# Mask and first score tables in SyncE's queue, swapped key halves of pair 0 on VectorE, and the exponential's function table ahead, in a two-layer diffusion step

## The chip, the cores and the metric

The kernel runs on one core of one Trainium2 chip. The time is device microseconds of one execution, the median of three runs. Engine names in the profile: PE is TensorE, DVE is VectorE, ACT is ScalarE, POOL is GpSimd, SP is SyncE, which only issues transfers; SPq and ACTq are issues of transfers by SyncE and by ScalarE.

## The reference

One step of a trunk with two layers, D = 1024, over 512 latent tokens (8 rows of 64) and 128 context tokens. Layer 0 mixes tokens by neighbourhood attention over 16 heads of 64, layer 1 by grouped-query attention; each is followed by a gated ConvFFN with 2816 hidden columns. Norms and adaptive shift, scale and gate stand around all of them. The change lies in layer 0's attention:

```python
qs, ks_, vs = na_qkv(hs, na_w_qkv[i])
...
bias = rpb[:, dr[:, None, :, None], dc[None, :, None, :]].astype(jnp.float32)
s_lat = jnp.where(col_ok[None, None, None, :, None, :], s_lat + bias[None], -jnp.inf)
s_ctx = jnp.einsum('brqhd,bchd->bhrqc', qg, k_ctx).astype(jnp.float32) * scale
s = jnp.concatenate([s_lat.reshape(b, h, rows, GRID_W, n_lat), s_ctx], axis=-1)
p = jax.nn.softmax(s, axis=-1).astype(v.dtype)
```

A latent token sees all 8 rows, 16 columns around its own, with a learned bias by relative position (`rpb`, per head), and the 128 cached context keys.

## The kernel before, in words

The 640 tokens (512 latent, 128 context) stand transposed in `hT`, as a high and a low part. Each weight tile of 512 KB is loaded by SyncE into one of four `wr` buffers, cast by ScalarE to a high part `wh`, and the remainder `wl` is made by VectorE or GpSimd (`wsplit`, L166 to L180); three matmuls, (high, high), (high, low) and (low, high), stand for one in full precision.

Stages at the start: loads, norms and modulation columns; values of heads 0 to 3 (`v_part`, until about 53 us); then queries and keys by pairs of heads. `na_qk_items(p)` gives pair `p` two loads (`load_q`, `load_k`) and 16 `part`s, 8 for queries and 8 for keys, each six matmuls into a bank `qk`. Of a key bank, `k_put` makes for each head of the pair a tile `kh` whose own 64 rows and whose other 64 rows (the swapped half) both hold the high part, and a tile `kl` with the low part in its own rows. `load_q` also loads cached keys `kc`.

`stream()` runs these items one after the other. After 20 parts (`PRO`: pair 0, and the first half of pair 1's queries) the first head is begun. `Head(h)` calls `na_table(h)`: three transfers, issued by ScalarE, fetch runs of the bias into `tr` (one buffer), and GpSimd makes the table `tb` from `mask` and `tr` in three operations. There are two `tb` buffers, for even and odd heads. `scores(slot)` is a pair of matmuls `s`, a VectorE operation that adds the table and finds the extreme `nm`, an exponential on ScalarE into `p`, a reciprocal `rc` on VectorE and a scaling of `p` on GpSimd. `turns` transposes `p` on TensorE (`tp`). Between the scores, further `part`s fill TensorE. `ada_work` streams modulation weights beside it, into two buffers of its own.

A scheduler of the language lays down the order of each engine's stream from the program, and sets semaphores; an engine works its stream in order, so an instruction that waits holds all behind it. Issues of transfers stand in the stream of the engine that issues them. `tc.add_manual_dep(..., no_sync)` fixes an order without a wait; all of TensorE's instructions are chained so (`pe`). A transfer also waits for the one before it on its semaphore, of which there are eight.

Of the kernel before, what the change touches and what calls it, by code (L numbers as in the profile page):

```python
# [19 lines left out]
P = 128  # L20
D = 1024
# [13 lines left out]
RPAD = 32  # L35
RLEN = 15 * 31 + 2 * RPAD
RUN = 8 * 31 + 1
# [35 lines left out]
def raw_ap(ap, offset, dims):  # L73
    return bass.AP(tensor=ap.tensor, offset=ap.offset + offset, ap=[list(d) for d in dims])
# [30 lines left out]
def hybrid_step(ctx: ExitStack, tc: tile.TileContext, A, O):  # L105
    nc = tc.nc
    no_sync = mybir.DependencyInfo(mybir.DependencyClass.NoSync, mybir.DependencyReason.DATA)
# [11 lines left out]
    def turn(*a, **k):  # L119
        pe(nc.tensor.transpose(*a, **k))  # L120

    def f32(t):
        return t.bitcast(F32)

    def pool(name, bufs=1, side="left", **k):
        return tc.tile_pool(name=name, bufs=bufs, side=side, reuse_waits="tile", **k)

    cst = ctx.enter_context(pool("cst"))
    wp = ctx.enter_context(pool("wp", 4))
    sm = ctx.enter_context(pool("sm", 4))  # L130
# [18 lines left out]
    mhalf = cst.tile([P, 1], F32, name="mhalf")  # L149
# [12 lines left out]
    def x_in(t):  # L162
        return A["x_sample"][0, t * P : (t + 1) * P, :] if t < 4 else A["x_prompt"][0]


    def wsplit(src, a, b, low=None, own=None, pin=False, after=None):  # L166
        q = own or wp
        raw = wp.tile([P, a, b], F32, tag="wr", name="wr")
        nc.sync.dma_start(raw, src)
        hi = q.tile([P, a, b], F32R, tag="wh", name="wh")  # L170
        i = nc.scalar.copy(hi, raw)  # L171
        lo = q.tile([P, a, b], F32R, tag="wl", name="wl")
        j = (low or nc.vector).tensor_sub(lo, raw, f32(hi))  # L173
        if after:
            behind(i, after[0])
            behind(j, after[1])
        if pin:
            tc.keep_in_program_order(i)
            tc.keep_in_program_order(j)
        return hi, lo  # L180

    def rows(w, r0, nr, c0, ncol):
        return w[r0 * P : (r0 + nr) * P, c0 : c0 + ncol].rearrange("(k p) n -> p k n", p=P)
# [81 lines left out]
    def ada_work(p, rawp, group, steps, todo, wait=1, sizes=()):  # L265

        bias = p.tile([P, 256], F32, name="abias")
        gr = p.tile([P, 256], F32, name="again")  # L270
        nc.gpsimd.memset(bias, 0.0)
        nc.gpsimd.memset(gr, 0.0)

        def quarters(row):
            return row.rearrange("(j c) -> j c", j=4)

        loads = deque((l, idx, k) for l, idx in todo for k in range(KC))
        raws = deque()

        def load():  # L280
            if loads:
                l, idx, k = loads.popleft()
                raw = rawp.tile([P, D], F32, tag="wr", name="wr")
                nc.sync.dma_start(raw, A["ada_w"][l, k * P : k * P + P, idx * D : idx * D + D])
                raws.append((l, idx, k, raw))

        for _ in range(group):
            load()
        for _ in range(wait):
            yield  # L290
        sizes = iter(sizes)
        while raws:
            n = min(len(raws), next(sizes, len(raws)))
            for _ in range(n):
                l, idx, k, raw = raws.popleft()
                if k == 0:
                    for q in range(2):
                        nc.sync.dma_start(bias[q::32, :], quarters(A["ada_b"][l, idx * D : idx * D + D]))
                        if idx in gain_of:
                            nc.sync.dma_start(gr[q::32, :], quarters(A[gain_of[idx]][l]))  # L300
                    ps = bk.get("ada")
                for j in range(4):
                    mm(ps[32 * j : 32 * j + 32, 0:256], scolp[:, 2 * k : 2 * k + 32], raw[:, 256 * j : 256 * j + 256],
                       start=k == 0, stop=k == KC - 1)
                if k < KC - 1:
                    continue
                orow = p.tile([P, 256], F32, tag="arow", name="arow")
                nc.vector.tensor_add(orow, ps[:, 0:256], bias)
                bk.put(ps)
                if idx in gain_of:  # L310
                    nc.vector.scalar_tensor_tensor(
                        orow, orow, 1.0 if idx in (1, 4) else 0.0, gr, op0=ALU.add, op1=ALU.mult
                    )
                for q in range(2):
                    nc.scalar.dma_start(quarters(modrow[l][idx][q]), orow[q::32, :])
            for i in range(steps):
                for _ in range(n if steps == 1 else i < n):
                    load()
                yield
# [144 lines left out]
    hT = new_hT(r_h0.enter_context(pool("h0", 1, "right")))  # L464
    l_na = ExitStack()
    vpool = l_na.enter_context(pool("nav", 3))
    wqkv = A["na_w_qkv"][0]

    def na_v_tile():
        return vpool.tile([P, 6, 4, HD], F32, tag="vt", name="vt", bufs=2)  # L470

    def na_v_put(vt, c, src):
        nc.scalar.copy(vt[:, c], src.rearrange("p (a d) -> p a d", a=4))

    def na_v_cache(vts, g):
        vc = vpool.tile([P, 256], F32, tag="vc", name="vc", bufs=1)
        nc.scalar.dma_start(
            vc, A["cache_na_v"][0, 0][:, 4 * g : 4 * g + 4, :].rearrange("t h d -> t (h d)")
        )
        na_v_put(vts, 5, vc)  # L480

    def na_v_out(g, src):
# [6 lines left out]
    vts_of, normed = {}, []  # L489
    with ExitStack() as s:  # L490
# [114 lines left out]
        vb = [bk.get("vp") for _ in range(NT)]  # L605
# [39 lines left out]
        v_part(6, range(NT))  # L645
        for c in range(NT):
            v_part(7, (c,))
            na_v_put(vts_of[0], c, vb[c][:, 0:256])
            if c == 4:
                na_v_out(0, vb[c][:, 0:256])  # L650
            bk.put(vb[c])

# [51 lines left out]
            nc.scalar.copy(hi, raw)  # L704
            return nc.vector.tensor_sub(lo, raw, f32(hi))

    def behind(ins, other):
        tc.add_manual_dep(ins.ins, other.ins.name, no_sync, reason="order")

    class Mix:  # L710


# [45 lines left out]

    with l_na:
        ap = l_na.enter_context(pool("na", 2))  # L760
        mask = ap.tile([P, 2, 32, 8], F32, name="mask", bufs=1)
        nc.scalar.dma_start(mask, A["k_mask"])
        tbs = [ap.tile([P, 7, P], F32, name=f"tb{i}", bufs=1) for i in range(2)]
        for tb in tbs:
            nc.gpsimd.memset(tb[:, 3, :], 0.0)
# [33 lines left out]
        def na_qk_items(p):  # L799
            d = {}  # L800

            def load_q():
                d["w"] = wsplit(rows(wqkv, 0, 8, P * p, P), 8, P, nc.gpsimd if p else None, after=None if p else normed)
                kc = ap.tile([P, P], F32, tag="kc", name="kc", bufs=2)
                nc.scalar.dma_start(
                    kc, A["cache_na_k"][0, 0][:, 2 * p : 2 * p + 2, :].rearrange("t h d -> t (h d)")
                )
                d["kc"] = kc

            def load_k():  # L810
                d["wk"] = wsplit(rows(wqkv, 0, 8, 1024 + P * p, P), 8, P, nc.gpsimd if p else None)

            def k_put(c0, c1, src):
                for b in range(2):
                    own, oth = own_oth(b)
                    nc.scalar.copy(d["kh"][b][own, c0:c1], src[own])
                    nc.scalar.copy(d["kh"][b][oth, c0:c1], src[own])
                    nc.vector.tensor_sub(d["kl"][b][own, c0:c1], src[own], f32(d["kh"][b][own, c0:c1]))

            def part(which, half, k0):  # L820
                w = d["w"] if which == 0 else d["wk"]
# [61 lines left out]
            return v6[:, 0:5:2, :] if slot == 0 else v6[:, slot - 1 : slot + 2, :]  # L883

        def na_table(h):
            tr = ap.tile([P, 2, RUN], F32, tag="tr", name="tr", bufs=1)
            base = h * RLEN + RPAD
            for dst, off, n in ((tr[:, 0, :], -8, 16), (tr[0:64, 1, :], 8, 8), (tr[64:128, 1, :], -16, 8)):
                nc.scalar.dma_start(dst, raw_ap(A["k_rpb"], base + off, [[1, n], [31, 8], [1, RUN]]))
            tb = tbs[h % 2]  # L890
            for w, dst in ((1, tb[:, 0::6, :]), (0, tb[:, 1:3, :]), (0, tb[:, 4:6, :])):
                t0 = tr[:, w, :]
                rv = raw_ap(t0, RUN - 1, [t0.ap[0], [-16, 2], [-1, 16], [-31, 8]])
                nc.gpsimd.tensor_sub(
                    dst.rearrange("p c (a b) -> p c a b", b=8),
                    mask[:, w].rearrange("p (c a) b -> p c a b", c=2), rv,
                )
            return tb
# [132 lines left out]
        for h in range(H):  # L1031
            nxt = Head(h + 1) if h + 1 < H else None
            g = h // 4
            pr = h % 4 == 1
            order = (ORDER if h < 13 else ORDER2)[h % 2] if h else ORDER0
            for i, step in enumerate(order):
# [402 lines left out]
    wqkv = A["gqa_w_qkv"][0]  # L1439
# [309 lines left out]
    for hq in range(2):  # L1749
        for n, t in enumerate(((4, 0, 1, 2, 3), (0, 1, 2, 3, 4))[hq]):  # L1750
# [3 lines left out]
            i = 5 * hq + n  # L1754
# [169 lines left out]
```

## Time and profile before

| | us |
|---|---|
| median of three runs | 1574.69 (1573.96 to 1576.03) |
| the profiled execution, its time | 1575.78 |
| its span | 1573.9 |
| PE busy | 1523.1 |
| DVE, ACT, POOL busy | 1029.7, 860.2, 699.5 |
| mean granted clock of PE | 0.99 |

The profiled execution is one run; its time is 1.88 us more than the span that the trace covers. In a row of a timeline stand the start, the duration, engine, line, operation, `out<-in` with sizes, how many (`x2`), and in brackets how long the engine had been idle and what ended it. Rows of waits give who waited for whom, the total in us, the number of times and the longest. Rows by windows give, after the stretch and its length, the busy time of PE, PEld, DVE, ACT and POOL, then the granted clock of PE, the busy share of the transfer engines, and GB/s.

### The profile page before, as it was taken

The numbers are of one execution on the slowest core, as the hardware profiler recorded it, in microseconds if no ns is written. First come the engines' busy times: TensorE is split into PE (matmuls) and PEld (weight loads), VectorE is DVE, ScalarE is ACT, GpSimd is POOL, SyncE is SP. The second block draws the span as 40 slices with busy tenths as digits, with TensorE's granted clock in tenths as the row PEclk, the third lists the DMA queues.
The fourth block names the chain that finished last, engine by engine and source line by source line (L and its number), as shares of the span: only waits on it lengthen the run. The fifth ranks groups of instructions, "written<-read, shape, count | busy, mean of one in ns | idle before, by whom it ended". The sixth has DMA issues, their size and how long they took to land.

```text
span 1573.9 us, 26057 instructions
## 1 busy us (share of the span) xinstructions
PE 1523.1 (97%) x9709; PEld 1351.0 (86%) x9709; DVE 1029.7 (65%) x1654; ACT 860.2 (55%) x1641; POOL 699.5 (44%) x606
## 2 busy tenths in 40 slices
PE   6799999999999999999999999999999999999998
PEld 4789899788999999978887777877899999988886
DVE  4353433649877666856757867773888887786554
ACT  4474655636655555554545436763666665554443
POOL 1455554422355555524444453542325566553433
PEclk9999999999999999999999998999999999999999
DMA  9745454245466665387574211004633334448664
GB/s 296 202 110 144 126 147 120 76 140 168 151 227 186 218 193 153 116 276 267 183 226 148 83 64 49 1 1 156 206 116 114 106 111 150 133 155 270 213 221 135
DMA packets 193211, 242.41 MB, mean 154 GB/s; under 512 B 11101, under 2 KB 149565, under 8 KB 193085
## 3 DMA queue, kind: packets, MB, share of 16 engines
q1 hardware_dynamic: 182224, 233.13, 46.2%
q10 hardware_dynamic: 10860, 7.62, 2.9%
q8 instruction: 76, 1.25, 0.3%
q14 instruction: 51, 0.41, 0.1%
HBM read 214.38 MB, written 26.34 MB: 153 GB/s over the span
## 4 chain that ended last, share of the span: by engine, by line
PE 61%; DVE 7%; ACT 2%; issue 2%; POOL 2%; DMA 2%; ACTq 0%; POOLq 0%; DVEq 0%; SPq 0%
PE acc L117 19%; PE ux L117 18%; PE uz L117 8%; PE uy L117 4%; PE y L117 2%; PE po L117 2%; PE s L117 2%; PE gp L117 2%; PE tp L120 2%; PE ada L117 1%; DMA wr<-in_ffn_w_up 1%; DVE wl L173 1%; DVE t L1244 1%; DMA gn<-in_gqa_k_norm 1%; DVE gkl L1527 1%
## 5 line engine op out<-in xcount | busy, mean ns | idle before, releaser
L173 POOL TENSOR_TENSOR wl<-wr,wh 128x1024 fp32r<-128x1024 f32 x70 | 171.7, 2455 | 237.9 <-ACT wh L171 223.0
L1167 POOL TENSOR_TENSOR wl<-wr,wh 128x1024 fp32r<-128x1024 f32 x76 | 183.4, 2435 | 48.3 <-ACT wh L1166 44.7
L117 PE MATMUL ux<-B,wh 128*128 128x322 f32 x832 | 200.1, 311 | 0.9 <-ACT u L1221 0.9
L1244 DVE SCALAR_TENSOR_TENSOR t<-C,cw,t 128x644 f32<-128x644 f32 x176 | 156.2, 888 | 51.3 <-ACT t L1242 50.7
L117 PE MATMUL acc<-wh,alo 128*128 128x512 f32 x440 | 172.3, 392 | 0.3 <-DVE alo L1136 0.3
L117 PE MATMUL acc<-wl,ahi 128*128 128x512 f32 x440 | 172.0, 391 | 0.0
L117 PE MATMUL acc<-wh,ahi 128*128 128x512 f32 x440 | 171.9, 391 | 0.0
L171 ACT CAST wh<-wr 128x1024 fp32r<-128x1024 f32 x140 | 145.4, 1048 | 43.8 <-DMA wr<-in_ffn_w_down 34.2
L117 PE MATMUL uz<-B,wh 128*128 128x322 f32 x640 | 156.2, 312 | 1.4 <-ACT v L1221 1.4
L117 PEld LDWEIGHTS ux<-B,wh 128*128 128x128 f32 x832 | 143.6, 189 | 3.3 <-ACT u L1221 1.6
L1136 DVE TENSOR_TENSOR alo<-ain,ahi 128x384 fp32r<-128x384 f32 (+1 forms) x88 | 83.9, 973 | 83.1 <-ACT ahi L1134 79.4
L117 PE MATMUL ux<-B,wl 128*128 128x322 f32 x416 | 129.5, 311 | 2.7 <-DVE wl L1167 2.7
L117 PE MATMUL qk<-hT,wh 128*128 128x384 f32 (+1 forms) x512 | 123.7, 318 | 0.0
L117 PEld LDWEIGHTS uz<-B,wh 128*128 128x128 f32 x640 | 110.9, 189 | 4.9 <-ACT v L1221 2.0
L1167 POOL TENSOR_TENSOR vl<-wr,vh 128x1024 fp32r<-128x1024 f32 x38 | 95.9, 2523 | 24.6 <-ACT vh L1166 24.3
L173 DVE TENSOR_TENSOR wl<-wr,wh 128x1024 fp32r<-128x1024 f32 x70 | 92.9, 1338 | 20.7 <-ACT wh L171 20.2
L1166 ACT CAST wh<-wr 128x1024 fp32r<-128x1024 f32 x84 | 84.8, 1049 | 39.7 <-DVE wr L1190 39.4
L1242 ACT ACTIVATE t<-C,cw 128x644 f32<-128x644 f32 x88 | 78.6, 893 | 48.5 <-DVE C L1272 40.9
L117 PE MATMUL uz<-B,wl 128*128 128x322 f32 x320 | 99.6, 311 | 0.3 <-POOL wl L1167 0.3
L117 PEld LDWEIGHTS acc<-wh,alo 128*128 128x128 f32 x440 | 82.5, 188 | 18.8 <-DVE alo L1136 1.1
L117 PEld LDWEIGHTS acc<-wl,ahi 128*128 128x128 f32 x440 | 82.6, 188 | 18.3 <-POOL wl L173 0.4
L117 PEld LDWEIGHTS acc<-wh,ahi 128*128 128x128 f32 x440 | 82.6, 188 | 17.6
(256 smaller groups left out, 3884.9 us busy)
## 6 DMA issues: line engine op xcount, KB each, us to landing
wr<-in_ffn_w_up SPq DMA_DIRECT2D x88, 512.0 KB
wr<-in_ffn_w_down SPq DMA_DIRECT2D x88, 512.0 KB
wr<-in_ada_w SPq DMA_DIRECT2D x72, 512.0 KB
act<-act SPq DMA_DIRECT2D x44, 321.0 KB
wr<-in_na_w_qkv SPq DMA_DIRECT2D x24, 512.0 KB
mod<-modrow SPq DMA_DIRECT2D x20, 512.0 KB
ain<-act SPq DMA_DIRECT2D x44, 192.0 KB
wf<-in_ada_w SPq DMA_DIRECT2D x16, 512.0 KB
```

The lines of the kernel that those rows point to most:

```text
L117: pe(nc.tensor.matmul(*a, **k))
L120: pe(nc.tensor.transpose(*a, **k))
L171: i = nc.scalar.copy(hi, raw)
L173: j = (low or nc.vector).tensor_sub(lo, raw, f32(hi))
L1136: pin(nc.vector.tensor_sub(lo[:, 0 : c1 - c0], ain[:, 0 : c1 - c0], f32(hi[:, 0 : c1 - c0])))
L1166: nc.scalar.copy(hl[0], src)
L1167: low.tensor_sub(hl[1], src, f32(hl[0]))
L1242: nc.scalar.activation(t, taps(0), AF.Identity, bias=cw[:, 3, n : n + 1], scale=cw[:, 1, n : n + 1])
L1244: nc.vector.scalar_tensor_tensor(t, taps(d), cw[:, w, n : n + 1], t, op0=ALU.mult, op1=ALU.add)
L1527: nc.vector.tensor_sub(kl[part, b::2, cols], tv[own], f32(kh[own, b::2, cols]))
```

## The change

Four edits, all around the first two heads.

The mask gets memory of its own from the start (`tpool`, apart from the attention's pool), and is loaded by SyncE behind pair 0's key weights. Tables 0 and 1's runs are loaded behind it by SyncE as well, table 0 into a `tr` buffer of `tpool`, table 1 into one of the four `wr` buffers (`na_runs`). The next three weight loads of SyncE are ordered behind them (`queue`). Table 2's runs, the cached values of the second group and the casts of pair 2's weights are ordered behind the last own-half key copy of pair 0 (`kput`); ScalarE issues runs for heads from 2 on, as before. In `k_put`, for pair 0 alone, VectorE makes the swapped halves in ScalarE's place. A one-element exponential behind the first group's values brings the function table load forward.

```diff
+    queue = []
...
-        nc.sync.dma_start(raw, src)
+        i = nc.sync.dma_start(raw, src)
+        if queue:
+            behind(i, queue.pop())
...
+        if high:
+            behind(i, high[0])
...
+    tpool = l_na.enter_context(pool("nat"))
+    mask = tpool.tile([P, 2, 32, 8], F32, name="mask")
+    kput = []
...
+        if g == 1:
+            behind(i, kput[0])
...
+        behind(nc.scalar.activation(sm.tile([P, 1], F32, name="ss"), mhalf, AF.Exp), i)
...
-        mask = ap.tile([P, 2, 32, 8], F32, name="mask", bufs=1)
-        nc.scalar.dma_start(mask, A["k_mask"])
+        runs = {}
+
+        def na_runs(h, q=nc.scalar):
+            if h == 1:
+                tr = wp.tile([P, 2, RUN], F32, tag="wr", name="tr")
+            else:
+                tr = tpool.tile([P, 2, RUN], F32, tag="tr", name="tr", bufs=1)
+            runs[h] = tr
+            base = h * RLEN + RPAD
+            for dst, off, n in ((tr[:, 0, :], -8, 16), (tr[0:64, 1, :], 8, 8), (tr[64:128, 1, :], -16, 8)):
+                i = q.dma_start(dst, raw_ap(A["k_rpb"], base + off, [[1, n], [31, 8], [1, RUN]]))
+                if h == 2:
+                    behind(i, kput[0])
+            return i
...
-                d["wk"] = wsplit(rows(wqkv, 0, 8, 1024 + P * p, P), 8, P, nc.gpsimd if p else None)
+                d["wk"] = wsplit(rows(wqkv, 0, 8, 1024 + P * p, P), 8, P, nc.gpsimd if p else None, high=kput if p == 2 else None)
+                if not p:
+                    nc.sync.dma_start(mask, A["k_mask"])
+                    for h in range(2):
+                        i = na_runs(h, nc.sync)
+                    queue.extend([i] * 3)
...
-                    nc.scalar.copy(d["kh"][b][own, c0:c1], src[own])
-                    nc.scalar.copy(d["kh"][b][oth, c0:c1], src[own])
+                    i = nc.scalar.copy(d["kh"][b][own, c0:c1], src[own])
+                    (nc.scalar.copy if p else nc.vector.tensor_copy)(d["kh"][b][oth, c0:c1], src[own])
...
+                if not p:
+                    kput[:] = [i]
```

Where it moves instructions. On SyncE, behind the last modulation loads (`wf`), stand before the weights of pair 0 (two) and pair 1 (two), two modulation loads, and pair 2's:

```order
L545 DMA wf<-in_ada_w 128x4x256 x4
L169 DMA wr<-in_na_w_qkv 128x8x128 x4
L284 DMA wr<-in_ada_w 128x1024 x2
L169 DMA wr<-in_na_w_qkv 128x8x128 x2
L298 DMA abias<-in_ada_b 4x256
```

Now:

```order
L561 DMA wf<-in_ada_w 128x4x256 x4
L174 DMA wr<-in_na_w_qkv 128x8x128 x2
L840 DMA mask<-in_k_mask 128x512
L785 DMA tr<-in_k_rpb 128x1x249
L785 DMA tr<-in_k_rpb 64x1x249 x2
L785 DMA tr<-in_k_rpb 128x1x249
L785 DMA tr<-in_k_rpb 64x1x249 x2
L174 DMA wr<-in_na_w_qkv 128x8x128
L293 DMA wr<-in_ada_w 128x1024
L174 DMA wr<-in_na_w_qkv 128x8x128
L293 DMA wr<-in_ada_w 128x1024
L174 DMA wr<-in_na_w_qkv 128x8x128
```

Seven transfers now stand between pair 0's and pair 1's weights, and modulation loads alternate with what follows.

On ScalarE, from pair 0's second query copies (384 columns) to its last key copies (`kh`), a part of the stream before:

```order
L889 DMA tr<-in_k_rpb 128x1x249
L889 DMA tr<-in_k_rpb 64x1x249
L843 ACTIVATE qs_668<-qk 64x64
L889 DMA tr<-in_k_rpb 64x1x249
L843 ACTIVATE qs_669<-qk 64x64
...
L889 DMA tr<-in_k_rpb 128x1x249
L889 DMA tr<-in_k_rpb 64x1x249 x2
L858 COPY kp<-qk 128x128
L816 CAST kh_740<-qk 64x384
L817 CAST kh_740<-qk 64x384
```

The same place now, up to the first exponential `p`:

```order
L848 CAST kh_753<-qk 64x256
L848 CAST kh_753<-tk 64x128
L848 CAST kh_754<-tk 64x128
L848 CAST kh_754<-qk 64x256
L892 COPY kp<-qk 128x128
L848 CAST kh_753<-qk 64x384
L848 CAST kh_754<-qk 64x384
L178 CAST wh<-wr 128x1024
L877 ACTIVATE qs_833<-qk 64x256
L178 CAST wh<-wr 128x1024
L966 ACTIVATE p,su<-s,nm 128x384
```

No `tr` issue is left ahead of the key copies, one copy per head and piece is gone, and the two casts of pair 2's weights stand between the key copies and the first exponential.

On GpSimd, from the clearing of `kl` to the first scalings of `p`, the order before:

```order
L173 TENSOR_TENSOR wl<-wr,wh 128x1024
L271 MEMSET abias 128x256
L272 MEMSET again 128x256
L173 TENSOR_TENSOR wl<-wr,wh 128x1024
L894 TENSOR_TENSOR tb_611<-mask,tr 128x256 x2
L894 TENSOR_TENSOR tb_611<-mask,tr 128x2x128
L173 TENSOR_TENSOR wl<-wr,wh 128x1024
L894 TENSOR_TENSOR tb_612<-mask,tr 128x256 x2
L894 TENSOR_TENSOR tb_612<-mask,tr 128x2x128
L173 TENSOR_TENSOR wl<-wr,wh 128x1024
L894 TENSOR_TENSOR tb_611<-mask,tr 128x2x128
L937 TENSOR_SCALAR p<-p,rc 128x384
```

and now:

```order
L280 MEMSET abias 128x256
L281 MEMSET again 128x256
L927 TENSOR_TENSOR tb_615<-mask,tr 128x2x128
L927 TENSOR_TENSOR tb_615<-mask,tr 128x256 x2
L927 TENSOR_TENSOR tb_616<-mask,tr 128x2x128
L927 TENSOR_TENSOR tb_616<-mask,tr 128x256 x2
L180 TENSOR_TENSOR wl<-wr,wh 128x1024 x4
L970 TENSOR_SCALAR p<-p,rc 128x384 x4
L927 TENSOR_TENSOR tb_615<-mask,tr 128x256 x2
```

Both tables stand ahead of pair 1's `wl`, and the four `wl` of pairs 1 and 2 in a row ahead of the four scalings of head 0. TensorE's order is the same as before.

More of the change, by code (lines that the diff above doesn't have):

```diff
@@ L120, in turn, with behind @@
         pe(nc.tensor.transpose(*a, **k))
+    def behind(ins, other):
+        tc.add_manual_dep(ins.ins, other.ins.name, no_sync, reason="order")
     def f32(t):
@@ L163, in x_in, with wsplit @@
         return A["x_sample"][0, t * P : (t + 1) * P, :] if t < 4 else A["x_prompt"][0]
-    def wsplit(src, a, b, low=None, own=None, pin=False, after=None):
+    queue = []
+    def wsplit(src, a, b, low=None, own=None, pin=False, after=None, high=None):
         q = own or wp
         raw = wp.tile([P, a, b], F32, tag="wr", name="wr")
-        nc.sync.dma_start(raw, src)
+        i = nc.sync.dma_start(raw, src)
+        if queue:
+            behind(i, queue.pop())
         hi = q.tile([P, a, b], F32R, tag="wh", name="wh")
@@ L283, in load @@
                 raw = rawp.tile([P, D], F32, tag="wr", name="wr")
-                nc.sync.dma_start(raw, A["ada_w"][l, k * P : k * P + P, idx * D : idx * D + D])
+                i = nc.sync.dma_start(raw, A["ada_w"][l, k * P : k * P + P, idx * D : idx * D + D])
+                if queue:
+                    behind(i, queue.pop())
                 raws.append((l, idx, k, raw))
@@ L472, in na_v_put @@
     def na_v_put(vt, c, src):
-        nc.scalar.copy(vt[:, c], src.rearrange("p (a d) -> p a d", a=4))
+        return nc.scalar.copy(vt[:, c], src.rearrange("p (a d) -> p a d", a=4))
     def na_v_cache(vts, g):
         vc = vpool.tile([P, 256], F32, tag="vc", name="vc", bufs=1)
-        nc.scalar.dma_start(
+        i = nc.scalar.dma_start(
             vc, A["cache_na_v"][0, 0][:, 4 * g : 4 * g + 4, :].rearrange("t h d -> t (h d)")
         )
+        if g == 1:
+            behind(i, kput[0])
         na_v_put(vts, 5, vc)
@@ L647, in hybrid_step @@
             v_part(7, (c,))
-            na_v_put(vts_of[0], c, vb[c][:, 0:256])
+            i = na_v_put(vts_of[0], c, vb[c][:, 0:256])
             if c == 4:
@@ L705, in split @@
             return nc.vector.tensor_sub(lo, raw, f32(hi))
-    def behind(ins, other):
-        tc.add_manual_dep(ins.ins, other.ins.name, no_sync, reason="order")
     class Mix:
@@ L802, in load_q @@
             def load_q():
-                d["w"] = wsplit(rows(wqkv, 0, 8, P * p, P), 8, P, nc.gpsimd if p else None, after=None if p else normed)
+                d["w"] = wsplit(rows(wqkv, 0, 8, P * p, P), 8, P, nc.gpsimd if p else None, after=None if p else normed, high=kput if p == 2 else None)
                 kc = ap.tile([P, P], F32, tag="kc", name="kc", bufs=2)
@@ L885, in na_table @@
         def na_table(h):
[L886 to L889, printed above, removed]
+            if h not in runs:
+                na_runs(h)
+            tr = runs.pop(h)
             tb = tbs[h % 2]
```

## The prediction, made before the changed kernel ran

> **What bounds the kernel now.** I read the page's shares first, then TensorE's waits over the whole span, then, around the longest wait, the timelines of the engines that it hangs on.
>
> ```profile
> PE 1523.1 (97%) x9709; PEld 1351.0 (86%) x9709; DVE 1029.7 (65%) x1654; ACT 860.2 (55%) x1641; POOL 699.5 (44%) x606
> PE s L117 <- ACT kh L817: 8.6, 1, 8.6
> PE ct L120 <- DMA ident<-in_k_ident: 7.9, 1, 7.9
> ```
>
> TensorE is the bound: it is busy for 97% of the span. Its longest single wait, 8.6 us, is for the first score `s` of the first head, which waits for ScalarE's key copies at L817. The next row is the first transfer of the program. In TensorE's timeline the wait stands between these rows, and the windows show the granted clock (the column after the five engines):
>
> ```profile
> 66.91 0.45 PE L117 MATMUL qk<-hT,wh 128*128 128x384 f32 x2
> 69.83 0.28 PE L117 MATMUL qk<-hT,wh 128*128 128x256 f32 x1
> 78.69 0.69 PE L117 MATMUL s<-kh,qs 128*128 128x384 f32 x1 [8.58 <-ACT kh L817]
> 81.67 0.42 PE L120 MATMUL tk<-ident,kp 128*128 128x128 f32 x1
> 84.36 0.34 PE L117 MATMUL s<-kh,qs 128*128 128x384 f32 x1
> 85.78 0.34 PE L117 MATMUL s<-kh,qs 128*128 128x384 f32 x1
> 70.11:78.69 8.58, 0.00 (x1) 0.01 (x1) 1.89 (x7) 4.38 (x15) 3.79 (x4) 0.73 0.65 107
> 78.69:84.36 5.67, 5.67 (x17) 5.28 (x18) 2.88 (x8) 5.51 (x11) 3.77 (x3) 0.51 0.28 66
> ```
>
> The last key matmul of pair 0 is the first of the two that begin at 66.91. TensorE stops at 70.11 and starts again at 78.69. After the wait it runs 5.67 us at clock 0.51. What ScalarE does meanwhile:
>
> ```profile
> 60.66 2.10 ACTq L889 DMA_DIRECT2D tr<-in_k_rpb  x3
> 63.30 0.49 ACT L843 ACTIVATE qs<-qk 64x384 fp32r<-64x384 f32 x1 [5.72 <-DMA tr<-in_k_rpb]
> 70.39 0.22 ACT L843 ACTIVATE qs<-qk 64x64 fp32r<-64x64 f32 x1 [5.15 <-issue]
> 75.63 1.84 ACTq L889 DMA_DIRECT2D tr<-in_k_rpb  x3
> 77.52 0.27 ACT L858 COPY kp<-qk 128x128 f32<-128x128 f32 x1 [3.29 <-issue]
> 77.68 0.47 ACT L816 CAST kh<-qk 64x384 fp32r<-64x384 f32 x1
> 65.86 1.70 POOL L894 TENSOR_TENSOR tb<-mask,tr 128x256 f32<-128x256 f32 x2 [6.21 <-DMA tr<-in_k_rpb]
> 68.21 0.86 POOL L894 TENSOR_TENSOR tb<-mask,tr 128x256 f32<-128x256 f32 x1 [0.65 <-DMA tr<-in_k_rpb]
> 74.75 0.85 POOL L894 TENSOR_TENSOR tb<-mask,tr 128x256 f32<-128x256 f32 x1 [0.56 <-DVE kl L818]
> ```
>
> ScalarE stands three times (5.72, 5.15, 3.29 us) behind issues of `tr` loads in its own stream. There is one `tr` buffer: table 1's load waits until GpSimd has built table 0 (its last row ends at 69.07), table 2's until table 1 is built (75.60), and the key copies come behind both. The chain is load, build, load, build, copy, with nothing of TensorE in it.
>
> **The change part by part.** It takes those loads out of ScalarE's stream. SyncE issues the mask and tables 0 and 1, table 1 into a weight buffer; table 2's load stands behind the key copies.
>
> *First term: the wait.* ScalarE is then free when the keys come. The last key matmul ends by 67.36 at the latest (66.91 + 0.45); `kp` takes 0.27 and the own half 0.47 (rows above): 68.10. VectorE's swapped half is a form that the trace does not show. Its bounds are the same job on ScalarE, 0.47, and a wider VectorE copy from the same memory, 0.69; the low part behind it is 0.55:
>
> ```profile
> 78.16 0.47 ACT L817 CAST kh<-qk 64x384 fp32r<-64x384 f32 x1
> 78.67 0.55 DVE L818 TENSOR_TENSOR kl<-qk,kh 64x384 fp32r<-64x384 f32 x1 [3.98 <-ACT kh L817]
> 91.84 0.69 DVE L948 COPY pk<-tp 128x512 f32<-128x512 f32 x1
> ```
>
> So `kl` is ready between 69.12 and 69.34, both ahead of 70.11. I take all 8.58 us as gone; the slack is about 0.8 us. The other end is that some of the wait stays (first rival).
>
> *Second term: the low clock.* From 78.69 to 84.36 TensorE runs two rounds of a score pair and six projection matmuls, and one `tk` transposition. The next such round, at full clock, is 85.78 − 84.36 = 1.42 us. At full clock the stretch costs 2 x 1.42 + 0.1 for `tk` (its 0.42 at half clock would be 0.2 at most) = 2.94, so 5.67 − 2.94 = 2.73 us go too if there is no wait. The bounds are 0 (a wait long enough to lower the clock stays) and 2.73; I take 2.73, as the clock was 1.00 until the wait. The Trainium skill, "TensorE: Matmul & The Clock Gate", Part 1, says that the clock halves after an idle window of about 3.4 us and returns after about 3.4 us of work, at a phase that varies; by it this term is an estimate of 1.7 us and the sum would be 1.0 us smaller. Here the low clock lasted 5.67 us, and the measured stretch decides.
>
> *Third term: a new wait, on `tp`.* What is late next is the first transposition of probabilities:
>
> ```profile
> 87.90 1.14 POOL L937 TENSOR_SCALAR p<-p,rc 128x384 f32<-128x384 f32 x2
> 88.63 0.80 PE L120 MATMUL tp<-ident,p 128*128 128x128 f32 x4
> 78.66 1.04 ACT L171 CAST wh<-wr 128x1024 fp32r<-128x1024 f32 x1
> 69.03 2.37 POOL L173 TENSOR_TENSOR wl<-wr,wh 128x1024 fp32r<-128x1024 f32 x1
> ```
>
> `tp` follows the fourth score by 88.63 − 85.78 = 2.85 us, and already waits a little for the fourth `p` (0.80 us for four). It moves to 88.63 − 11.31 = 77.32. On GpSimd four `wl` now stand ahead of the four `p`, and the casts for the last two come behind the key copies. The first cast starts at about 69.6 (the second head's own half waits for the first's `kl`) and ends at 70.6, the second, after a query copy, at 72.0; their `wl` of 2.37 end at 73.0 and 75.4, four `p` of 0.57 at 77.7 to 78.2 (the last one also waits for ScalarE, which issues two table-2 loads of 0.6 us before the last exponential). The fourth transposition would start at 77.6. I take 0.5 us. The bounds are 0 and 2.4 (one `wl` late).
>
> *Terms that I take as zero, and their covers.*
>
> ```profile
> 37.25 8.51 SPq L169 DMA_DIRECT2D wr<-in_na_w_qkv  x4
> 52.07 1.51 SPq L169 DMA_DIRECT2D wr<-in_na_w_qkv  x2
> 40.00:50.00 10.00, 9.17 (x94) 7.56 (x94) 6.09 (x16) 5.32 (x10) 0.00 (x0) 1.00 1.15 282
> tr<-in_k_rpb ACTq DMA_DIRECT2D x16, 124.5 KB
> tr<-in_k_rpb ACTq DMA_DIRECT2D x32, 62.2 KB
> 51.22 3.07 POOL L769 MEMSET kl<- 64x768 f32 x4
> 56.61 0.30 POOL L271 MEMSET abias<- 128x256 f32 x1
> 67.20 0.27 PE L117 MATMUL qk<-hT,wl 128*128 128x256 f32 x1
> 87.30 0.28 PE L117 MATMUL qk<-hT,wl 128*128 128x256 f32 x1
> ```
>
> Seven transfers pass ahead of pair 1's weights in SyncE's queue: the mask (256 KB) and two tables of 249 KB, together 0.75 MB, or 2.7 us at the 282 GB/s of that stretch. Pair 1's query weights, issued within the 8.51 us from 37.25, then land near 53 to 55. On GpSimd their `wl` stands behind six table operations of 0.85: the memsets end at 54.3, the two small ones at 54.9, the tables at 60.0, `wl` at 62.4; TensorE asks for it at 67.20, so 4.8 us of cover. Pair 1's key weights now share a buffer with pair 0's query weights, since table 1 holds one of the four, so their issue moves to 52.07, where such a wait ended before. With 8 us to land, 1.04 and 2.37 they are ready by 65; TensorE asks at 87.30 − 11.31 = 76.0. Without that cover each us late is a us of TensorE.
>
> Table 2, for head 2, comes later than tables 0 and 1: its load is issued near 75.5, lands 5.2 us on (60.66 to 65.86 above), and its three operations, with a `wl` among them, end by 86; head 2's first score moves from 105.90 to 94.6.
>
> ```profile
> 105.90 0.42 PE L117 MATMUL s<-kh,qs 128*128 128x384 f32 x1
> 81.10 1.28 ACT L933 ACT_TABLE_LOAD   x1
> 55.86 0.38 ACT L843 ACTIVATE qs<-qk 64x256 fp32r<-64x256 f32 x1 [2.21 <-PE qk L117]
> 90.00:130.00 40.00, 39.74 (x316) 35.83 (x314) 20.31 (x60) 26.34 (x77) 21.32 (x22) 1.00 0.52 129
> ```
>
> The function table (1.28 us) moves from 81.10, inside the low-clock stretch, to about 53.5, where ScalarE had 2.21 us to spare. Behind it stand the cast and the query copies, wanted only by 70. The six swapped halves are 2.2 us that leave ScalarE for a VectorE that waits there. From 90 to 130 TensorE is busy for 39.74 of 40.00 us and no other engine for more than 26.34, so I expect the shift to carry to the end.
>
> *Sum.* −8.58 − 2.73 + 0.5 = −10.8 us. The profiled execution took 1575.78 us, 1.88 more than its span, and 1.09 more than the median of the three runs. Its span becomes 1563.1, its time 1565.0; against the median the forecast is 1574.69 − 10.8 = 1563.9 us.
>
> **The rivals.** *Part of the wait stays (same sign, smaller).* ScalarE is in order, and the two casts of pair 1's weights stand ahead of the first and second query copies. From the second cast to the last key copy lie some 5.5 us of its work and VectorE's, so from a landing after about 63 on, each us keeps one us of the wait. Against it: issue at 52.07. For it: transfers were saturated at 40 to 50 (share 1.15). With 3 to 5 us kept, the low clock may stay as well: 1567 to 1571 us.
>
> *The gain is given back.* An engine other than TensorE sets the pace of the heads, and the 11 us return as waits before 130: 1574.7 us. Against it are the 39.74 of 40.00 above.
>
> *Slower: weights late behind tables.* GpSimd holds pair 1's `wl` until both tables are loaded and built. If table 1 lands at 71 instead of about 52, its three operations end at 73.6 and `wl` at 76.0; TensorE stands 8.8 us at 67.2 and loses 2.7 more at the low clock, and the gain is used up. If it lands at 76, 13.8 + 2.7 are lost against 11.3, and the time is some 1580 us. For it: table 1's loads wait in a queue that also carries the weights. Against it: a table needed 5.2 us beside two weight loads, and a delay of 19 is asked for. The Trainium skill, "DMA: Bandwidth & Descriptors", Queues, rings and completion order, says that each issuing queue's descriptors are consumed in ring order on the same 16 engines; by that rule weights issued behind the tables land behind them.
>
> **How the numbers follow.** Forecast 0.72 (its own range 1562 to 1566: the sum with 0 to 2.4 for the third term), partial 0.16, given back 0.07, slower 0.05. A measurement of this kernel can tell about 0.2%, 3.1 us. Partial lies past that: faster 0.88, same 0.07, slower 0.05. The range takes in the forecast's and most of the partial case: 1561.8 to 1570.
>
> **What would show it.** TensorE's waits have no row for `s` on `kh` above 1 us; the windows from 70 to 90 show clock 1.00; ScalarE has no `tr` issue between 55 and 70; GpSimd's six table operations lie between 54 and 61; the first `s` starts near 70.1 and `tp` near 77.5 with up to 1 us of wait on `p`. A wait of TensorE at 67 or at 76 on `wl`, or a `CAST` of ScalarE held by a weight load past 63, would make it wrong.

## The result, and the profile after

The changed kernel takes 1567.5 us, median of six runs (1563.37 to 1568.93), against 1574.72 for the kernel before beside it (1573.59 to 1576.03): ratio 0.9948, 95% interval [0.9935, 0.9962]. The forecast was 1563.9 us, faster, range 1561.8 to 1570. The sign and the range held; the median lies above the forecast's own range of 1562 to 1566. The gain is 7.2 us by these medians where 10.8 were forecast, and, as the experiments show, it is made up otherwise than the sum said.

The profiled execution of the changed kernel took 1564.15 us, 1.75 more than its span of 1562.4; it lies 3.35 us under the median. A line of its page, its waits of TensorE (who waits for whom, us in total, times, longest), and one row of the waits of before that the prediction did not use:

```profile
PE 1518.7 (97%) x9709; PEld 1347.9 (86%) x9709; DVE 1028.1 (66%) x1660; ACT 858.4 (55%) x1636; POOL 700.2 (45%) x606
```

```profile
PE ct L120 <- DMA ident<-in_k_ident: 7.3, 1, 7.3
PE tp L120 <- POOL p L970: 4.5, 5, 2.9
PE row L117 <- DMA wf<-in_ada_w: 0.2, 1, 0.2
```

```profile
PE row L117 <- DMA wf<-in_ada_w: 2.6, 4, 0.9
```

The wait of `s` for `kh`, 8.6 us before, has no row any more. A row is new: `tp` waits for GpSimd's `p` (L970 is L937 of before), 2.9 us at once. The wait of the first modulation matmuls (`row`) for `wf`, 2.6 us before, is nearly gone, though no edit touches those transfers. TensorE's timeline of the changed kernel, from the first score `s` to head 1's transpositions:

```profile
66.86 0.34 PE L117 MATMUL s<-kh,qs 128*128 128x384 f32 x1
69.90 0.33 PE L117 MATMUL s<-kh,qs 128*128 128x384 f32 x1
74.16 0.27 PE L120 MATMUL tp<-ident,p 128*128 128x128 f32 x1
75.81 0.42 PE L117 MATMUL s<-kh,qs 128*128 128x384 f32 x1
92.53 0.38 PE L120 MATMUL tp<-ident,p 128*128 128x128 f32 x2
95.85 1.03 PE L120 MATMUL tp<-ident,p 128*128 128x128 f32 x2 [2.94 <-POOL p L970]
96.54 0.67 PE L117 MATMUL s<-kh,qs 128*128 128x384 f32 x1
99.21 0.33 PE L117 MATMUL s<-kh,qs 128*128 128x384 f32 x1
```

The next rows are of the timelines, each kernel's own: first a value matmul at the start and the instructions at the new wait in before, then the same value matmul after:

```profile
43.89 0.39 PE L117 MATMUL vp<-wh,hT 128*128 128x256 f32 x1
105.55 0.60 PE L120 MATMUL tp<-ident,p 128*128 128x128 f32 x4
107.38 0.34 PE L117 MATMUL s<-kh,qs 128*128 128x384 f32 x1
```

```profile
40.79 0.38 PE L117 MATMUL vp<-wh,hT 128*128 128x256 f32 x1
```

TensorE's order is the same in both kernels, so the start of one and the same instruction, after less before, shows where time comes from. The 78.69, 84.36 and 88.63 of before stand in the prediction; 89.18 is the score behind head 0's first `tp`.

| instruction | before | after | difference | what the step is |
|---|---|---|---|---|
| third group of value matmuls | 43.89 | 40.79 | −3.10 | the start |
| first `s`, head 0 | 78.69 | 66.86 | −11.83 | the wait: −8.73 |
| third `s`, head 0 | 84.36 | 69.90 | −14.46 | the low clock: −2.63 |
| first `s`, head 1 | 89.18 | 75.81 | −13.37 | head 0's `tp` wait for `p`: +1.09 (+0.27 in a1_again, below) |
| first `tp`, head 1 | 105.55 | 92.53 | −13.02 | small waits: +0.35 |
| second `s`, head 2 | 107.38 | 99.21 | −8.17 | new: +4.85 |

From there the difference stays between −8.2 and −8.4 us up to 850 us. The windows of the changed kernel (busy time of PE, PEld, DVE, ACT, POOL, then the granted clock, the share of the transfer engines, GB/s) show the last step as a wait with a low clock behind it:

```profile
74.00:90.00 16.00, 15.20 (x112) 13.39 (x111) 8.36 (x25) 11.45 (x31) 7.68 (x9) 1.00 0.64 180
90.00:94.00 4.00, 2.91 (x19) 2.64 (x18) 0.43 (x1) 0.00 (x0) 3.59 (x4) 1.00 0.02 6
94.00:98.00 4.00, 2.06 (x7) 1.77 (x8) 1.72 (x5) 3.12 (x12) 2.58 (x4) 0.72 0.75 111
98.00:102.00 4.00, 4.00 (x29) 3.97 (x28) 2.70 (x8) 3.15 (x7) 3.30 (x4) 0.86 0.34 101
```

What GpSimd, ScalarE and SyncE did meanwhile (their timelines, in that order):

```profile
51.53 5.03 POOL L927 TENSOR_TENSOR tb<-mask,tr 128x256 f32<-128x256 f32 x6
81.57 0.85 POOL L927 TENSOR_TENSOR tb<-mask,tr 128x256 f32<-128x256 f32 x1
90.41 2.53 POOL L927 TENSOR_TENSOR tb<-mask,tr 128x256 f32<-128x256 f32 x3 [6.85 <-DMA tr<-in_k_rpb]
92.90 2.34 POOL L180 TENSOR_TENSOR wl<-wr,wh 128x1024 fp32r<-128x1024 f32 x1
95.21 1.15 POOL L970 TENSOR_SCALAR p<-p,rc 128x384 f32<-128x384 f32 x2
82.45 1.87 ACTq L785 DMA_DIRECT2D tr<-in_k_rpb  x3
94.27 0.27 ACT L903 COPY ko<-tk 128x128 f32<-128x128 f32 x1 [4.85 <-issue]
82.28 1.21 SPq L293 DMA_DIRECT2D wr<-in_ada_w  x2
```

This is table 3, for head 3. Heads from 2 on share one `tr` buffer, so ScalarE issues table 3's runs when table 2's last operation (81.57 + 0.85) is done. In that moment SyncE issues 1 MB of modulation weights. The runs land 6.1 us after their last issue (84.32 to 90.41). GpSimd stands 6.85 us with head 1's last two `p` behind the table in its stream, and ScalarE stands behind table 4's issue. No one needs table 3 yet; TensorE needs the `p`. In before, the three pieces of the same load were issued at 89.62, 90.27 and 93.25, ahead of the modulation weights, and had landed 2.8 us after the last issue (93.85 to 96.69); its timelines of ScalarE, SyncE and GpSimd:

```profile
89.62 0.58 ACTq L889 DMA_DIRECT2D tr<-in_k_rpb  x1
90.27 0.62 ACTq L889 DMA_DIRECT2D tr<-in_k_rpb  x1
93.25 0.60 ACTq L889 DMA_DIRECT2D tr<-in_k_rpb  x1
95.29 0.82 SPq L284 DMA_DIRECT2D wr<-in_ada_w  x2
96.69 0.88 POOL L894 TENSOR_TENSOR tb<-mask,tr 128x256 f32<-128x256 f32 x1 [2.72 <-DMA tr<-in_k_rpb]
```

So table 3's runs were issued 7.2 us (first piece) to 9.5 us (last) earlier than in before and landed 6.3 us earlier, while TensorE came to head 1's `tp` 13.0 us earlier: the loads through the one buffer did not keep up with it. Had the runs landed 2.8 us after their last issue here too, they would have been there 3.2 us sooner, about the length of the wait. That the modulation weights held them is argued from this; no run moved those weights alone.

The last 3 us by which this execution ends ahead (span 1573.9 to 1562.4 is 11.5, not 8.4) come at 880 to 950 us, where TensorE's granted clock falls in some executions and in others not:

```profile
890.00:897.00 7.00, 6.47 (x18) 5.31 (x19) 5.55 (x13) 3.61 (x11) 3.08 (x3) 0.53 0.01 2
```

```profile
882.00:886.00 4.00, 3.61 (x18) 3.06 (x19) 3.85 (x10) 0.76 (x2) 2.87 (x3) 1.00 0.02 6
```

The first row is of before, the second of after, a little earlier in time and at the same matmuls. In a second execution of the changed kernel (a1_again, below) the clock from 880 to 884 is 0.59. So this part is a draw of the execution, and I compare traces ahead of it and whole kernels by runs.

### The profile page after: what moved, and what is told of

It reads as the page before. It is cut to its first block, busy times and chain, and to the rows that moved or that the text cites. A ratio compares the mean times of both kernels' runs of the same rounds, so it can differ in the third digit from the quotient of the medians.

```text
span 1562.4 us, 26067 instructions
## 1 busy us (share of the span) xinstructions
PE 1518.7 (97%) x9709; PEld 1347.9 (86%) x9709; DVE 1028.1 (66%) x1660; ACT 858.4 (55%) x1636; POOL 700.2 (45%) x606
## 3 DMA queue, kind: packets, MB, share of 16 engines
q10 hardware_dynamic: 10140, 6.85, 2.5%
q8 instruction: 76, 1.25, 0.3%
## 4 chain that ended last, share of the span: by engine, by line
PE 62%; DVE 7%; ACT 2%; issue 2%; POOL 2%; DMA 2%; ACTq 0%; POOLq 0%; DVEq 0%; SPq 0%
PE acc L117 19%; PE ux L117 18%; PE uz L117 8%; PE uy L117 4%; PE y L117 2%; PE po L117 2%; PE s L117 2%; PE tp L120 2%; PE gp L117 2%; PE ada L117 1%; DMA wr<-in_ffn_w_up 1%; DVE wl L180 1%; DVE t L1277 1%; DMA gn<-in_gqa_k_norm 1%; DVE gkl L1560 1%
```

## Experiments

The ratios are to the kernel before, run on the same chip beside each.

**Is the new wait a fault of the program?** a1_again is the changed kernel, unedited.

> The changed kernel once more, unedited. In its first profile TensorE waits 2.94 us at 92.9 us for GpSimd's p before head 1's first tp, and is 4.85 us later behind it (with the half clock that follows) than in the kernel before. Theory A (a fault of the program: GpSimd stands behind table 3, whose runs land late): the wait comes again, 2.5 to 3.5 us at the same tp, median 1566 to 1568.5 us. Rival R (an accident of that run, and the give-back comes from elsewhere): no wait above 1 us there, the median nearer 1564. Also open: the first profile started 3.1 us ahead of before by TensorE's first value matmuls; if that is a draw of the run, this trace starts within 1 us of before's.

Measured: 1566.38 us (1562.94 to 1567.84), before 1574.61, ratio 0.9945 [0.9932, 0.9959].

```profile
PE tp L120 <- POOL p L970: 3.5, 3, 3.0
```

```profile
880.00:884.00 4.00, 3.17 (x10) 2.71 (x11) 3.87 (x9) 0.33 (x1) 2.42 (x3) 0.59 0.02 4
```

The wait comes again, 3.0 us at head 1's `tp` (the first row is of TensorE's waits from 66 to 130 us, the second of the windows). Theory A holds, rival R falls. The start is again early (2.9 us at the same value matmul): not a draw.

**Table 3 asked for earlier.** e1_two_runs has two `tr` buffers (one `pk` buffer less makes the room), and asks for each table from 3 on one table earlier:

```diff
-NPK = 6
+NPK = 5
...
-                tr = tpool.tile([P, 2, RUN], F32, tag="tr", name="tr", bufs=1)
+                tr = tpool.tile([P, 2, RUN], F32, tag="tr", name="tr", bufs=2)
...
-            return tb
+            return (2 <= h < H - 1 and na_runs(h + 1), tb)[1]
```

> The changed kernel with two tr buffers and the runs of each head from 3 on asked for one table earlier (pk buffers 5 in place of 6 to make room). Theory A (table 3's late landing, issued only after table 2 was built and behind 1 MB of modulation weights, holds wl and p in GpSimd's order): the 2.94 us wait at head 1's tp goes, with the half clock behind it; 4.5 to 5 us faster than the changed kernel, about 1562.7 us. Rival B (GpSimd's work itself, tables plus two wl ahead of p, is too much in that stretch): 2 us or more of the wait stay, about 1566 to 1567.

Measured: 1564.64 us (1564.09 to 1566.25), ratio 0.9941 [0.9928, 0.9954]. TensorE's waits from 60 to 130 us, and GpSimd's timeline at table 3:

```profile
PE tp L120 <- POOL p L970: 0.2, 1, 0.2
```

```profile
83.65 0.87 POOL L927 TENSOR_TENSOR tb<-mask,tr 128x256 f32<-128x256 f32 x1
87.50 1.71 POOL L927 TENSOR_TENSOR tb<-mask,tr 128x256 f32<-128x256 f32 x2 [0.62 <-DVE nm L962]
91.52 1.15 POOL L970 TENSOR_SCALAR p<-p,rc 128x384 f32<-128x384 f32 x2
```

The wait is gone; table 3 no longer waits for its load. In TensorE's timeline e1 gains 4.6 us on a1_again between the first `s` and 220 us, as theory A said. The time fell by only 1.7 us to 1564.64, not to the 1562.7 expected: e1 lost 2.15 us at its start, whose transfers were back at before's rate (below), and the intervals of the two overlap.

**Only the order on GpSimd.** e2_p_first puts table 3 behind head 1's last `p`:

```diff
+                h == 3 and behind(j, lastp[1])
```

(`j` is each of table 3's operations, `lastp[1]` the last scaling of head 1.)

> The changed kernel with only the order on GpSimd edited: table 3's three operations stand behind head 1's last two p. Loads and buffers as they are. Theory A (the load's lateness reaches TensorE only because p stands behind the table in GpSimd's order): the wait at head 1's tp goes, 4.5 to 5 us faster than the changed kernel, about 1562.7 us, unless head 3's first score then waits for its table. Rival B (p is late by itself, from rc or the wl ahead): the wait keeps 2 us or more, about 1566 to 1567. Rival C (the wait is passed on: table 4's loads on ScalarE wait for table 3 and hold head 2's exponentials): a new wait of 2 to 3 us at a later tp, 1565 to 1567.

Measured: 1565.51 us (1564.12 to 1566.0), ratio 0.9943 [0.9931, 0.9955]. TensorE's waits from 60 to 130 us:

```profile
PE po L117 <- DVE qs L878: 1.7, 1, 1.7
PE s L117 <- DVE qs L878: 0.9, 1, 0.9
PE tp L120 <- POOL p L971: 0.2, 1, 0.2
```

The wait on `p` is gone, so the order on GpSimd is what carried the late load to TensorE. But 2.6 us of other waits come behind it, for VectorE's `qs`. ScalarE, which makes the first part of `qs`, stands behind table 4's issue, and that issue waits for table 3, now built last (ScalarE's timeline):

```profile
94.12 0.37 ACT L689 ACTIVATE pp<-sp,nmp 128x128 f32<-128x128 f32 x1 [3.18 <-POOL tb L927]
```

The 0.9 us at `s` follow from this; the 1.7 us at `po` come 6 us later and were not followed back. The wait is passed on, as rival C said (I expected it at a later `tp`; it is at `s` and `po`). Asking earlier is the better cure: in TensorE's timeline, from the first `s` to 120 us, e1 gains 4.9 us on a1_again and e2 2.4.

**The loads undone.** u1_runs_scalar lets ScalarE issue tables 0 and 1 again, into one buffer; the order of table 2's runs behind the key copies goes with it. The rest is kept:

```diff
-            if h == 1:
-                tr = wp.tile([P, 2, RUN], F32, tag="wr", name="tr")
-            else:
+            if True:
...
-                if h == 2:
-                    behind(i, kput[0])
...
-                    for h in range(2):
-                        i = na_runs(h, nc.sync)
-                    queue.extend([i] * 3)
```

> The changed kernel with the loads of tables 0 and 1 undone: ScalarE issues them again, into one tr buffer; the mask on SyncE, VectorE's swapped halves and the early function table stay. The prediction's first term (the loads in ScalarE's stream make the wait of the first s): 7 to 9 us of wait at the first s return, with the half clock, and the time is 1572 to 1576 us. Rival (the mask's own memory, the halves and the function table carry a good part): a wait of 3 to 5 us, 1568 to 1571.

Measured: 1571.74 us (1568.41 to 1574.66, 12 runs), ratio 0.9983 [0.9974, 0.9991].

```profile
74.44 0.69 PE L117 MATMUL s<-kh,qs 128*128 128x384 f32 x1 [5.09 <-DVE kh L842]
```

The wait returns, but with 5.1 us, less than the 7 to 9 of the first theory and just above the rival's 3 to 5. So the loads in ScalarE's stream do make the wait. With them there, the rest of the change is worth some 3.5 us of it; what of the rest was not separated (the place of the tiles at the start, below, is part of it: alone it gave 6.7 us of wait in one trace and 8.5 in another, for 8.6). With the loads moved, the halves and the function table bring nothing that the runs resolve, as the next two show.

**The halves and the function table undone, each alone.** u2_halves_scalar puts the swapped halves back on ScalarE, u3_no_table_ahead takes the early exponential out:

```diff
-                    (nc.scalar.copy if p else nc.vector.tensor_copy)(d["kh"][b][oth, c0:c1], src[own])
+                    nc.scalar.copy(d["kh"][b][oth, c0:c1], src[own])
```

```diff
-        behind(nc.scalar.activation(sm.tile([P, 1], F32, name="ss"), mhalf, AF.Exp), i)
```

> The changed kernel with VectorE's swapped halves undone: ScalarE makes all twelve copies of pair 0's keys. The prediction took the halves as bought for nothing (2.2 us that leave ScalarE, slack 0.8 us): by it the first s waits 0 to 1.5 us and the time is the changed kernel's to 1.5 us longer, 1566 to 1568. Rival Q (u1_runs_scalar kept 3.5 us of the gain without SyncE's loads, so the halves carry a good part): 2 to 3.5 us of wait at the first s, 1568.5 to 1570.

> The changed kernel without the early exponential: the function table (1.28 us) is loaded again ahead of the first head's first exponential. The prediction took this edit as free and without effect on the end. By its third term, four p that end with TensorE's tp already waiting 0.6 to 1.1 us, they come up to 1.3 us later: 0.5 to 1.5 us longer than the changed kernel. Rival: GpSimd's two wl end last there, so nothing changes, within 0.5 us.

Measured: u2 1564.72 us (1563.37 to 1567.15), ratio 0.9937 [0.9925, 0.995], no wait of `s` on `kh`; u3 1565.73 us (1563.33 to 1566.03), ratio 0.9939 [0.9926, 0.9951]. Neither is slower than the changed kernel. The prediction's zero for both held; rival Q fell, and for u3 the price of 0.5 to 1.5 us that I had expected did not show. In u3 the wait at head 1's `tp` was 1.7 us in place of 2.9, with another order on GpSimd; why was not followed further.

**Why the start is faster.** In the changed kernel 20 to 40 us move more than before: this window of before, of after and of e1_two_runs, in that order.

```profile
20.00:40.00 20.00, 17.52 (x178) 12.58 (x177) 10.31 (x25) 10.04 (x17) 0.00 (x0) 0.93 1.09 348
```

```profile
20.00:40.00 20.00, 18.03 (x204) 13.59 (x206) 12.23 (x29) 10.83 (x18) 0.00 (x0) 1.00 1.10 378
```

```profile
20.00:40.00 20.00, 17.00 (x184) 12.71 (x182) 11.04 (x27) 10.76 (x18) 0.00 (x0) 1.00 1.09 348
```

The transfer engines are saturated in all three (1.09, 1.10), with the same transfers in the same order. What differs there is where the tiles lie: the change opens `tpool` under the pool of the start, which holds the inputs and the first modulation weights, and so shifts these by 4064 bytes. b1_empty_4k adds to the kernel before only that shift:

```diff
+    empty = ExitStack()
+    empty.enter_context(pool("nat")).tile([P, 1010], F32, name="empty")
...
+        empty.close()
         ap = l_na.enter_context(pool("na", 2))
```

> The kernel before with nothing added but 4 KB per partition of empty memory at the place where the change puts the mask and the first tr buffer, given back before the attention's pool opens. Open is why the changed kernel's traces run 3 us ahead of before's already at 44 us: the transfers from 20 to 40 us go at 384 GB/s there, at 348 in before and in e1_two_runs. Theory M (memory: where the tiles of the start lie sets that rate): 384 GB/s here too, no wait of TensorE for wf above 0.4 us in total, values of the first group 2 to 3 us earlier, and the time 0 to 3 us shorter, as ScalarE's chain of loads may take the gain up. Theory D (a draw of each run): the rate is 348 or 384 by chance and the time is before's, within 1.5 us.

Measured: 1570.51 us (1567.43 to 1572.08, 8 runs), ratio 0.9971 [0.996, 0.9981]. Empty memory alone gives 4.1 us by the medians, half of the changed kernel's gain or more. It is more than the 0 to 3 us of theory M: in the trace the start came 2.1 us earlier, and the wait at the first `s` was 6.7 us in place of 8.6. b2 and b3 are the same with 32 and 224 bytes (`[P, 8]` and `[P, 56]`):

> The kernel before with 32 bytes per partition of empty memory at the place where b1_empty_4k had 4064. By the programs, the first modulation weights (wf) go to byte 127264 of a partition in before and 133344 in e1_two_runs (348 GB/s; 32 and 224 past a multiple of 256, both 32 past one of 64), and to 131328, a multiple of 256, in all kernels with 384 GB/s. Here they go to 127296, a multiple of 64 but 64 past one of 256. Theory 64 (rows that begin at a multiple of 64 bytes go faster): 384 GB/s from 20 to 40 us, 3 to 4.5 us less than before. Theory 256 (a row of 1024 bytes off a multiple of 256 takes one piece more): 348 GB/s, before's time within 1 us. Theory S (it is the 4 KB, not the alignment): 348 and before's time, here and in b3_empty_224.

> As b2_empty_32 with 224 bytes: wf goes to 127488, a multiple of 256 (and of 512). Theories 64 and 256: 384 GB/s from 20 to 40 us and 3 to 4.5 us less than before, as b1_empty_4k (1570.5). Theory S: 348 GB/s and before's time.

Measured: b2 1574.7 us (1572.92 to 1578.7, 11 runs), ratio 0.9997 [0.9988, 1.0006]; b3 1571.86 us (1569.41 to 1573.71, 10 runs), ratio 0.9977 [0.9967, 0.9988]. The same window of b1, b2 and b3:

```profile
20.00:40.00 20.00, 18.02 (x192) 13.93 (x194) 11.80 (x28) 10.84 (x18) 0.00 (x0) 1.00 1.09 378
```

```profile
20.00:40.00 20.00, 17.66 (x180) 12.73 (x179) 10.70 (x26) 10.28 (x17) 0.00 (x0) 0.94 1.10 348
```

```profile
20.00:40.00 20.00, 18.02 (x188) 13.88 (x186) 11.72 (x28) 10.78 (x18) 0.00 (x0) 1.00 1.09 380
```

Of the three theories only the one on 256 bytes gives all the rates: on a multiple of 256 the rate is 378 to 380 GB/s in this window, 32, 64 and 224 bytes past it 348. (128 would do as well; no run told the two apart.) In b3's trace the start came 2.0 us earlier, but the wait at the first `s` stayed at 8.5 us, so b1's shorter wait is not a sure part of the gain.

The reason that the theory gives, one piece more for each row, is not shown, and one reading speaks against it. In the same stretch come two loads of value weights with rows of 1024 bytes too; by the programs, their tiles lie 224 bytes past a multiple of 256 in every kernel. Counted by packets in the queue's order, the first of them goes at 385 GB/s in after and at 349 in before, as its neighbours do. So the place of the start's pool sets the rate of the whole stretch, and how it does so stays open.

**The edits without the placement.** a2_off_256 is the changed kernel with 32 bytes of empty memory more:

```diff
-    mask = tpool.tile([P, 2, 32, 8], F32, name="mask")
+    mask, _ = tpool.tile([P, 2, 32, 8], F32, name="mask"), tpool.tile([P, 8], F32, name="empty")
```

> The changed kernel, order and work unedited, with 32 bytes of empty memory behind the mask, so that wf goes to byte 131360, 32 past a multiple of 256, as in before. It shows what the four edits are worth without the faster start. Theory M (placement gives about 3.1 us of the gain, the edits the rest: 8.7 and 2.6 taken, 1.4 and 4.9 given back, so about 5.1): 348 GB/s from 20 to 40 us, the first s near 70 us, and a time 4.5 to 6 us less than before's, a ratio near 0.997. Rival E (the edits alone give the whole gain of 7 to 9 us, and the start's gain would have been taken up by the later waits): a ratio near 0.9945, with less wait at head 1's tp.

Measured: 1568.98 us (1567.22 to 1571.64), before 1574.92, ratio 0.9964 [0.9951, 0.9976].

```profile
20.00:40.00 20.00, 17.87 (x180) 12.81 (x179) 10.73 (x26) 10.41 (x17) 0.00 (x0) 0.93 1.09 348
```

```profile
69.53 0.34 PE L117 MATMUL s<-kh,qs 128*128 128x384 f32 x1
97.47 0.33 PE L120 MATMUL tp<-ident,p 128*128 128x128 f32 x1 [2.82 <-POOL p L970]
```

Theory M: 5.9 us by the medians, 4.5 to 6 expected; the first `s` starts at 69.53, the wait at head 1's `tp` is 2.8 us, as in the changed kernel. So the four edits are worth some 6 us, and the rest of the changed kernel's gain is placement: 1.5 to 2.6 us by the medians of its two sets of runs. The intervals of the ratios overlap (0.9951 to 0.9976 here, 0.9932 to 0.9962 there), so for this part the traces are the better witness: at 850 us TensorE is 6.6 us ahead of before here, 8.4 and 8.7 in the two traces of the changed kernel.

**Both together.** e3_two_runs_moved is e1 with the second `tr` buffer in the attention's pool, so that the start keeps its placement (and table 3's runs, like table 2's, behind the key copies):

```diff
-                tr = tpool.tile([P, 2, RUN], F32, tag="tr", name="tr", bufs=2)
+                tr = (tpool if h % 2 or not h else ap).tile([P, 2, RUN], F32, tag="tr", name="tr", bufs=1)
...
-                if h == 2:
+                if h in (2, 3):
```

> e1_two_runs with the same order on every engine, but the second tr buffer in the attention's pool, so that the memory of the start lies as in the changed kernel. Theory M: 384 GB/s from 20 to 40 us, the first s near 67 us, the wait at head 1's tp gone as in e1: 1561 to 1562.5 us, faster than the changed kernel and than e1. Theory D: as e1_two_runs, 1564 to 1565, at 348 or 384 by chance.

Measured: 1562.64 us (1561.49 to 1563.29, 4 runs), ratio 0.9922 [0.9908, 0.9935], with 379 GB/s from 20 to 40 us and no wait on `p` above 0.2 us. It is 12.0 us under before's median, and the lowest of all medians here; the interval of its ratio just touches those of the changed kernel. e4_p_before_wl sets pair 2's two `wl` behind head 0's four `p` on GpSimd:

```diff
-                d["wk"] = wsplit(rows(wqkv, 0, 8, 1024 + P * p, P), 8, P, nc.gpsimd if p else None, high=kput if p == 2 else None)
+                d["wk"] = wsplit(rows(wqkv, 0, 8, 1024 + P * p, P), 8, P, nc.gpsimd if p else None, after=(kput[0], lastp[0]) if p == 2 else None)
```

(the same in `load_q`; `lastp[0]` is the last scaling of head 0.)

> e3_two_runs_moved with one order on GpSimd edited: pair 2's two wl (4.76 us) stand behind head 0's four p in place of ahead of them. The prediction's third term says that these wl make TensorE wait at the first tp: in the changed kernel's first trace it lost 1.1 us there, in e3 about 0.4 us. Theory (the wl ahead of p): the wait there ends, 0.3 to 1.1 us less than e3's 1562.6. Rival (the last exponential, behind ScalarE's issues of table 2, ends last): no change, within 0.3 us; if the wl then come late for pair 2 or for table 2, up to 2 us more.

Measured: 1563.48 us (1560.6 to 1565.02), ratio 0.9921 [0.9907, 0.9936]. No wait on `p` is left, and TensorE gains 0.43 us on e3 between 60 and 76 us, as the theory's lower end said; in the time it does not show.

## Why the prediction was right, and where not

*First and second term: right, in mechanism and size.* The wait went as a whole: 8.73 us against 8.58, and the low clock behind it 2.63 against 2.73. u1 ties it to the loads in ScalarE's stream. The estimate of 1.7 us after the Trainium skill, "TensorE: Matmul & The Clock Gate", Part 1, was the worse one.

*Third term.* 1.09 us at head 0's `tp` and 0.35 behind it, against 0.5 within bounds of 0 to 2.4; in a1_again, the same kernel, only 0.27 at that `tp`, so the size varies from one execution to another. The reason given, two `wl` ahead of the `p` on GpSimd, is borne out by e4 for the 0.4 us that e3 still lost there.

*Zero terms.* TensorE waited for no weight at 67 or 76 us. GpSimd's six table operations lie at 51.5 to 56.6 (54 to 61 expected). Table 2 was built by 82.4, before the 86 of the prediction. Halves and function table cost and bring nothing that the runs resolve (u2, u3).

*The step that failed* is the last of the sum: "I expect the shift to carry to the end", from 39.74 busy us of 40 in the mean of 90 to 130. I followed table 2 to where it is wanted and stopped there. Table 3 comes through the same buffer, 10 us later; its load was issued only 7.2 to 9.5 us earlier than in before where TensorE came 13.0 us earlier, it was under way together with the modulation weights, and it landed 6.3 us earlier. GpSimd, with head 1's last `p` behind table 3 in its stream, passed that on: 4.85 us given back, 2.94 as a wait and 1.9 at the low clock. e1 and e3 ask for the table earlier, and the wait is gone. That is the second rival in part; I had given it 0.07, and only for the whole gain. The 39.74 of 40.00 us are a mean of before; they say nothing of what is late once TensorE comes earlier.

*The step that was missing* is the start. The new `tpool` also moves the pool of the start, and the sum has no term for that. It was worth 2 to 2.5 us at TensorE's value matmuls (in after's own execution 3.10, of which 0.58 was an earlier first instruction), and about 4 us of time in the kernel before (b1, b3); the traces show 2 of these at the start and 1 to 2 at the first `s`, in b1 mostly as a shorter wait, in b3 as a shorter stretch of low clock.

Against the sum of −10.8 stands −8.73 − 2.63 + 1.09 + 0.35 + 4.85 = −5.1 for the edits (a2: −5.9 by medians) and −3.1 for the start: −8.2 together, where the two sets of runs gave −7.2 and −8.2. So the range held on a sum with two errors of opposite sign, which is luck as far as the number goes; the edits alone (a2, 1568.98 us) would have lain inside the range too, near its upper end.

*Small slips, without weight.* The terms as written, with 0 to 2.4 for the third, give 1563.4 to 1565.8, not down to 1562. And `ident` is not the first transfer of the program: SyncE issues it sixth.

## What to carry to other kernels

When a wait of 10 us is taken away, follow each shared buffer behind it through at least two more uses: the next loads through it may come forward by less than their user does (here 6 us against 13), and meet other transfers than they did before. In an in-order stream, work that nobody waits for yet must not stand ahead of work that TensorE waits for; but an early request is better than a late place. After any edit that adds or moves on-chip memory, compare the rate of the first saturated stretch of transfers: here a shift of 32 bytes cost the changed kernel 1.5 to 2.6 us (a2), where all four edits bring some 6.

## What the runs showed of the hardware

The rate of the transfers at the start depends on the byte at which the tiles of the start's pool begin. With 16 transfer engines saturated, a multiple of 256 gave 378 to 384 GB/s (20 to 40 us; a packet of 1024 bytes took 46 ns in after), and 32, 64 and 224 bytes past one gave 348 each (51 ns, the median in before). Why is open. The Trainium skill, "DMA: Bandwidth & Descriptors", How a descriptor splits into AXI transactions, says of what a descriptor reads that its first transaction begins at the boundary of 256 bytes below, if it does not start on one. By it, carried over to the tile that is written, as an estimate, a row of 1024 bytes takes five transactions in place of four at every offset. The traces agree in that all offsets cost alike, but the rates differ by 1.09, not by 1.25; by its count of beats, 33 at an offset of 32 and 39 at one of 224 in place of 32, they should cost differently, and here they do not. And the value weights, 224 bytes past a multiple in every kernel, went at 385 GB/s in after.

A wait of 2.94 us was enough for the low clock: the window from 94 to 98 was granted 0.72, and 1.9 us of the 4.85 were lost behind the wait, not in it. After the waits of 0.9 and 1.7 us in e2 the clock stayed at 1.00 (92 to 110 us).
